# A hybrid decoder layer in float32: other pairs of products in the down projection, its sums on VectorE, and float32 sums at the FFN's entry

## The chip, the core and the metric

One core of one Trainium2 chip runs the whole layer in one launch. The metric is the time of the program on the device in microseconds (us). Of the core's engines, TensorE (PE) multiplies matrices into PSUM, VectorE (DVE) and ScalarE (ACT) work on SBUF and PSUM, GpSimd (POOL) on SBUF, and SyncE (SP) issues most of the transfers (DMA), in its program's order.

## What is computed

The reference is one layer over x, 1024 tokens of 1024 features, all in float32: a mixer of pooling and gated linear attention, an attention over 256 memory tokens, and a feed-forward network (FFN) with a causal convolution of width 3, each added to the residual, with a final norm. The change lies in the last part:

```python
h = rms_norm(x, norm_ffn_w)
u = h @ w_up                       # 1024 x 5632
u = conv_b + conv_w[0]*u_pad[:, 0:s] + conv_w[1]*u_pad[:, 1:1+s] + conv_w[2]*u_pad[:, 2:2+s]
x = x + (silu(u[..., :2816]) * u[..., 2816:]) @ w_down
return rms_norm(x, norm_final_w)
```

## The kernel before

**Three products for one.** Every float32 factor is held as a pair: `hi`, a copy rounded by ScalarE (L96, for weights L117), and `lo`, what is left, subtracted by VectorE (L97, L118). A product of two factors is three matmuls, hi·hi, lo·hi and hi·lo (`mm3c`, L888 to L892), of 128 x 128 by 128 x 512. A pair for the next product is called a unit.

**Seven block products for eight.** Both matrix products of the FFN cut their factors into two by two blocks and form seven products of sums of blocks. For the up projection the two halves of the tokens and of the features are the blocks, and the sums of activations are T1 to T4 and B22; for the down projection the two halves of 2816 inner features (11 blocks `k` of 128 each) and of 1024 outputs.

**The entry of the FFN.** Before the up projection, eight tiles of 128 tokens are normed (`normed`, L297) and transposed on TensorE (L829). The first four become pairs in H3. Of the other four `sums12` (L822) forms T1, T2 and B22, and `sums34` (L838) T3 and T4, out of the pairs: `whole` (L806) has GpSimd add hi and lo again (L811), and VectorE subtracts (L815). This runs beside the end of the attention's output projection and the first up jobs. `up_units` (L914) prepares the weight units of one of 22 blocks `f`, with sums of weights on GpSimd (L880, L883). The first three blocks are begun with two products each (`up_pre`, L949), then `up` (L967) does the other five; later blocks do all seven, 84 matmuls.

**The down projection** (`down`, L1083) goes over the 11 blocks k four times: products 1 and 2 in pass one, 6 and 5 in pass two, 3 and 7 in pass three, 4 in pass four. Each product of one k is four token tiles of three matmuls (`run`), so a pass has 264 matmuls, the fourth 132. Units come from `feed`, pass by pass; `take` keeps five of them ready. `units12` to `units4` load the gated activations (`G`, spilled to DRAM, as is the residual) and weights, form sums on GpSimd (`padd`, `psub`) or VectorE (`less`), and split them. Pass four loads its weights again (`wpair`). Finished sums go onto the residual R: the sums of one set of PSUM banks by VectorE (L877), the others by `spread`, a ScalarE copy and a GpSimd addition. During pass four the tiles 0 to 3 are normed and stored (L1128); the last two k of pass four run tile by tile, and tiles 4 to 7 are normed behind them, half by half (L1143 to L1150).

**What sets the order.** A scheduler fixes each engine's order of instructions when the program is built; SP's queue takes loads and stores in that order, and an instruction that waits holds all behind it on its engine. Buffers come from pools: two for raw weights of the down projection, four for hi and lo of units and eight more among the big ones, five and three PSUM banks.

Of the kernel before, what the change touches and what calls it, by code (L numbers as in the profile page):

```python
# [15 lines left out]
P = 128  # L16
# [26 lines left out]
def hybrid_layer(ctx: ExitStack, tc: tile.TileContext, x, mem, norm_mix_w, w_in, pool_w, pool_scale,  # L43
# [754 lines left out]

    for t in range(4):
        spill(t)  # L800
    finish(J["wo", 1, 0])
    B22 = Feat(TB, HK)
    for i in (1, 2):
        TT[i] = Feat(TB, HK)

    def whole(feat, k0, c0):  # L806

        r = t2(512).rearrange("p (k c) -> p k c", k=HK)
        for j in (0, 2):
            h = feat.slot(k0 + j)[:, :, c0:c0 + P]  # L810
            pin(nc.gpsimd.tensor_tensor(r[:, j:j + 2, :], h.hi.bitcast(F32), h.lo.bitcast(F32), ALU.add))  # L811
        return r

    def less(dst, a, b):
        nc.vector.tensor_tensor(dst, a, b, ALU.subtract)  # L815

    def tquad():
        return t2(512).rearrange("p (k c) -> p k c", k=HK)

    def sums12(xn, i, b11):  # L822

        c0 = i * P
        ps = []
        for q in range(2):
            p = bankB()
            for j in range(4):
                nc.tensor.transpose(p[:, j * P:(j + 1) * P], xn[:, (4 * q + j) * P:(4 * q + j + 1) * P], ident)  # L829
            ps.append(p.rearrange("p (k c) -> p k c", k=HK))  # L830
        less(b11, ps[0], b11)
        t = tquad()
        less(t, ps[1], b11)
        B22.put(0, HK, c0, P, ps[1])
        TT[2].put(0, HK, c0, P, t)
        TT[1].put(0, HK, c0, P, b11)

    def sums34(i):  # L838
        c0 = i * P
        t, b = whole(TT[2], 0, c0), whole(H3, 0, c0)  # L840
        less(b, t, b)
        TT[3].put(0, HK, c0, P, b)
        b = whole(H3, HK, c0)
        less(b, b, t)
        TT[4].put(0, HK, c0, P, b)

    plan[0].open = True
    b1 = whole(H3, 0, 0)
# [51 lines left out]
    def b11(k):  # L900
        return H3.k(k)
# [301 lines left out]
```

## Time and profile before

| | |
|---|---|
| median of three runs | 1356.41 us (1355.82 to 1357.3) |
| the profiled run | 1357.08 us, of which its span 1355.3 us |
| mean granted TensorE clock of the span | 0.978 of full |
| busy: TensorE, VectorE, ScalarE, GpSimd | 1288.3, 881.9, 640.5, 372.6 us |
| instructions: VectorE, ScalarE, GpSimd | 1248, 1150, 341 |
| moved by DMA | 149.71 MB, mean 110 GB/s |

The trace is of one execution. The views used are the stretches (busy time of each engine in stretches of the span, with granted clock), and the timeline (instructions in order of time, equal neighbours merged as x2, with the idle time ahead and what ended it). Matmuls are pipelined: a row's duration is longer than the distance of two starts. Pass one begins at 1084.24 us, pass two at 1147.60, pass three at 1233.54, pass four at 1296.07.

### The profile page before, as it was taken

The page shows a single profiled execution, that of the slowest core. Times are in us where ns is not written, and L with a number is a line of the kernel's source. Part 1 is how long each engine was busy: PE and PEld are TensorE (multiplying, and loading weights), DVE is VectorE, ACT ScalarE, POOL GpSimd, SP SyncE. Part 2 cuts the span into 40 slices and gives each one's busy share as a digit, 9 for nine tenths or more (in the row PEclk, how much of TensorE's full clock was granted, in tenths as well). Part 3 has the DMA queues.
Part 4 walks back from the last instruction along what each step waited for, and adds up shares of the span by engine and source line. Part 5 has one row for each costly group of instructions (what it writes and reads, how often), then busy time and mean ns, then how long its engine had stood idle before and what let it go on. Part 6 is the DMA issues. An engine that isn't in the chain of part 4 may idle for free. (4 is left out here: it accounts for less than half of the span.)

```text
span 1355.3 us, 17032 instructions
## 1 busy us (share of the span) xinstructions
PE 1288.3 (95%) x6326; PEld 1068.6 (79%) x6326; DVE 881.9 (65%) x1248; ACT 640.5 (47%) x1150; POOL 372.6 (27%) x341
## 2 busy tenths in 40 slices
PE   8999999999999999999789999999999999788975
PEld 7898878888778899988568888888888877676853
DVE  6623765237666544477877667766776674999565
ACT  6536444364455433354355545554555454234443
POOL 2000110001200000024844433444344302764273
PEclk9999999999999999999799999999999999899988
DMA  9333134322322222243123222222222477433333
GB/s 294 125 95 91 63 133 160 94 71 73 141 78 63 63 66 75 91 136 117 47 79 102 68 94 93 71 70 94 94 70 71 155 272 269 164 110 112 106 128 120
DMA packets 143521, 149.71 MB, mean 110 GB/s; under 512 B 4744, under 2 KB 112974, under 8 KB 143439
## 3 DMA queue, kind: packets, MB, share of 16 engines
q1 hardware_dynamic: 142431, 146.02, 33.5%
q0 software_dynamic: 432, 1.57, 0.4%
q8 instruction: 49, 0.80, 0.2%
q10 hardware_dynamic: 576, 1.05, 0.2%
q14 instruction: 33, 0.27, 0.1%
HBM read 128.70 MB, written 19.92 MB: 110 GB/s over the span
## 5 line engine op out<-in xcount | busy, mean ns | idle before, releaser
L118 DVE TENSOR_TENSOR wl<-wr,wh 128x512 fp32r<-128x512 f32 (+1 forms) x222 | 155.7, 702 | 209.6 <-ACT wh L117 204.9
L117 ACT ACTIVATE wh<-wr 128x512 fp32r<-128x512 f32 (+1 forms) x222 | 140.2, 632 | 285.8 <-PE pa L91 82.1
L890 PE MATMUL pa<-r,wh 128*128 128x512 f32 x400 | 159.6, 399 | 5.2 <-ACT f L886 5.2
L90 PE MATMUL pa<-wh,r 128*128 128x512 f32 (+2 forms) x480 | 159.1, 332 | 0.0
L891 PE MATMUL pa<-r,wh 128*128 128x512 f32 x400 | 158.9, 397 | 0.0
L892 PE MATMUL pa<-r,wl 128*128 128x512 f32 x400 | 158.2, 396 | 0.1
L92 PE MATMUL pa<-wh,r 128*128 128x512 f32 (+2 forms) x480 | 157.0, 327 | 0.2
L91 PE MATMUL pa<-wl,r 128*128 128x512 f32 (+2 forms) x480 | 157.2, 327 | 0.0
L90 PE MATMUL pa<-r,wh 128*128 128x512 f32 (+1 forms) x384 | 150.1, 391 | 0.7 <-ACT r L96 0.7
L92 PE MATMUL pa<-r,wl 128*128 128x512 f32 (+1 forms) x384 | 144.7, 377 | 0.3 <-DVE wl L118 0.3
L91 PE MATMUL pa<-r,wh 128*128 128x512 f32 (+1 forms) x384 | 144.6, 377 | 0.0
L92 PEld LDWEIGHTS pa<-wh,r 128*128 128x128 f32 x480 | 90.3, 188 | 9.4 <-DVE r L97 1.0
L90 PEld LDWEIGHTS pa<-wh,r 128*128 128x128 f32 x480 | 90.4, 188 | 7.8 <-ACT r L96 0.2
L91 PEld LDWEIGHTS pa<-wl,r 128*128 128x128 f32 x480 | 90.4, 188 | 7.7 <-issue 0.2
L963 DVE SCALAR_TENSOR_TENSOR f<-f,vec,f 128x1023 f32<-128x1023 f32 x44 | 86.8, 1975 | 14.5 <-ACT f L962 14.5
L890 PEld LDWEIGHTS pa<-r,wh 128*128 128x128 f32 x400 | 76.3, 191 | 25.2 <-ACT f L886 7.9
L117 ACT ACTIVATE wh<-ws 128x512 fp32r<-128x512 f32 x88 | 55.3, 629 | 80.4 <-PE pa L891 33.9
L892 PEld LDWEIGHTS pa<-r,wl 128*128 128x128 f32 x400 | 76.1, 190 | 17.9 <-DVE wl L118 0.4
L891 PEld LDWEIGHTS pa<-r,wh 128*128 128x128 f32 x400 | 76.2, 190 | 16.8
L892 PE MATMUL pb<-r,wl 128*128 128x512 f32 x216 | 85.9, 398 | 3.6 <-DVE wl L118 3.6
L890 PE MATMUL pb<-r,wh 128*128 128x512 f32 x216 | 86.1, 399 | 3.3 <-ACT wh L117 3.0
L891 PE MATMUL pb<-r,wh 128*128 128x512 f32 x216 | 85.9, 398 | 0.0
(215 smaller groups left out, 2828.8 us busy)
## 6 DMA issues: line engine op xcount, KB each, us to landing
wr<-in_ffn_w_up_dram SPq DMA_DIRECT2D x47, 512.0 KB, 3.7
wr<-in_ffn_w_down_dram SPq DMA_DIRECT2D x44, 512.0 KB, 4.2
wr<-in_w_in_dram SPq DMA_DIRECT2D x24, 512.0 KB, 4.0
gd<-f SPq DMA_DIRECT2D x22, 512.0 KB, 2.6
f<-gd SPq DMA_DIRECT2D x22, 512.0 KB, 5.8
f<-in_xattn_wkv_dram SPq DMA_DIRECT2D x16, 512.0 KB, 7.1
f<-in_x_dram SPq DMA_DIRECT2D x16, 512.0 KB, 7.3
wr<-in_w_out_dram SPq DMA_DIRECT2D x16, 512.0 KB, 3.6
```

The lines of the kernel that those rows point to most:

```text
L90: nc.tensor.matmul(ps, l.hi, r.hi, start=start, stop=False)
L91: nc.tensor.matmul(ps, l.hi, r.lo, start=False, stop=False)
L92: nc.tensor.matmul(ps, l.lo, r.hi, start=False, stop=stop)
L117: ia = nc.scalar.activation(w.hi, src, AF.Copy)
L118: ib = nc.vector.tensor_tensor(w.lo, src, w.hi.bitcast(F32), ALU.subtract)
L890: nc.tensor.matmul(ps, l.hi, r.hi, start=start, stop=False, **kw)
L891: nc.tensor.matmul(ps, l.hi, r.lo, start=False, stop=False, **kw)
L892: nc.tensor.matmul(ps, l.lo, r.hi, start=False, stop=stop, **kw)
L963: nc.vector.scalar_tensor_tensor(v[:, 1:], u[:, 0:T - 1], cw(1, f), v[:, 1:], ALU.mult, ALU.add)
```

## The change

**The FFN's entry.** A class `Blocks` takes the place of H3 and TT. The first four tiles' transposes become pairs, and ScalarE also copies them to SBUF in float32 (`half0`). The other four tiles' sums are formed from these copies and from PSUM by VectorE alone, in one pass per tile (`half1`); GpSimd adds no hi and lo any more. The pairs of T1, T3, B22 and T4 are split one name at a time over all four tiles (`split`). The up projection's weight sums of blocks 0 and 1 move from GpSimd to VectorE. The norm's 1/1024 goes into ScalarE's square.

**The down projection.** Passes are 1 and 5, 6 and 3, 7 and 2, then 4. All sums are VectorE's; GpSimd has none, and ScalarE one copy per k in pass two. Pass four loads and sums nothing: its operand is left over from pass three. Each set of banks is added to the residual by VectorE straight from PSUM (`onto`), at the end of every pass, and banks are used on. Two more buffers hold raw weights. The loads of the residual move into pass one, after k=5. The last four k, instead of two, run tile by tile, and in the final norm the sum of the two squares is one GpSimd addition with the small constant added by VectorE.

```diff
 def up_units(f, part):
+    q = nc.vector if f < 2 else nc.gpsimd
-    padd(st[1], st[21], st[22])
+    q.tensor_tensor(st[1], st[21], st[22], ALU.add)
...
-def sums12(xn, i, b11):
-def sums34(i):
+    def half0(self, i, xn):
+        r = f4(2, 512)
+        self.raw["T3", i], self.raw["T4", i] = r[:, 0], r[:, 1]
+        for q, p in enumerate(self.rows_T(xn)):
+            self.first.put(4 * q, 4, i * P, P, quad(p))
+            copy(r[:, q], p)
+    def half1(self, i, xn):
+        b12, b22 = self.rows_T(xn)
...
+        less(r[:, 0], b12, t3)
+        less(t, b22, r[:, 0])
+        self.done["T2"].put(0, HK, i * P, P, quad(t))
+        copy(r[:, 1], b22)
+        less(t3, t, t3)
+        less(t4, t4, t)
...
+def units15(k):
+    less(b12, b12, b11)
+    add(s1, g1[:, 1, :], g2[:, 1, :])
+    less(g1[:, 1, :], g1[:, 0, :], g1[:, 1, :])
+    less(g1[:, 0, :], g2[:, 1, :], g1[:, 1, :])
+def units63(k):
+    less(b12, b22, b12)
+    add(b12, b12, b11)
+    less(s4, g2[:, 0, :], g1[:, 0, :])
+    nc.scalar.activation(g1[:, 0, :], b12, AF.Copy)
+def units72(k):
+    less(b11, g1[:, 0, :], b11)
+    less(g1[:, 0, :], b21, g1[:, 0, :])
 def units4(k):
-    b11, b21 = wpair(k, 0)
-    psub(b21, b21, b11)
-    less(b21, b21, g1[:, 0, :])
-    yield unit(g2[:, 1, :]), unit(b21)
+    yield unit(a2[k][:, 1, :]), unit(a1[k][:, 0, :])
...
+    def onto(t0, hs, ps):
+        for t in range(4):
+            add(R[t0 + t][:, hs], ps[t], R[t0 + t][:, hs])
+    X, Y = banks(), banks()
+    yield from both(X, Y, True, True, residual)
+    onto(0, lo, X)
+    onto(4, hi, Y)
+    yield from both(X, Y, False, False)
+    onto(0, hi, X)
+    onto(0, hi, Y)
+    Z = banks()
+    yield from both(X, Z, False, True)
+    onto(4, hi, X)
+    onto(0, lo, Z)
+    for k in range(KH - LAST):
+        yield from run(X, False, False)
```

**Three places in the order.** In the rows below a line number, an operation and its tiles stand for each instruction; numbers behind a tile's letter tell one tile from another.

VectorE at the entry, where the last tile of tokens is summed, before. `wl` are the lo parts of weight units (the first two rows those of block 1), `r` lo parts of activations; L815 are sums:

```order
L118 TENSOR_TENSOR wl_6188<-wr_6185,wh_6187 128x512
L118 TENSOR_TENSOR wl_6192<-wr_6185,wh_6191 128x512
L815 TENSOR_TENSOR t_6138<-pb_6221,t_6138 128x512 [waits PE_49]
L118 TENSOR_TENSOR wl_6297<-wr_6294,wh_6296 128x512 [waits DMAHW2_49]
L815 TENSOR_TENSOR t_6232<-pb_6226,t_6138 128x512 [waits DVE_49,PE_49]
L97 TENSOR_TENSOR r_5881<-t_6138,r_5879 128x2x128 [waits Activation_49]
L97 TENSOR_TENSOR r_5882<-t_6138,r_5880 128x2x128 [waits Activation_49]
L97 TENSOR_TENSOR r_5877<-pb_6226,r_5875 128x2x128 [waits Activation_49]
L97 TENSOR_TENSOR r_5885<-t_6232,r_5883 128x2x128 [waits DVE_49,Activation_49]
L97 TENSOR_TENSOR r_5886<-t_6232,r_5884 128x2x128 [waits Activation_49]
L97 TENSOR_TENSOR r_5878<-pb_6226,r_5876 128x2x128 [waits Activation_49]
```

There the units of block 1 stand ahead of the last tile's sums. After, L800 are the sums, and the four lo parts `wl` at the end are those of blocks 1 and 2:

```order
L97 TENSOR_TENSOR r_6307<-f_5956,r_6305 128x2x128 [waits DMAHW2_49,Activation_49]
L800 TENSOR_TENSOR f_5814<-t_6216,f_5814 128x512 [waits DVE_49]
L97 TENSOR_TENSOR r_5944<-t_6216,r_5942 128x2x128 [waits Activation_49]
L97 TENSOR_TENSOR r_5945<-t_6216,r_5943 128x2x128 [waits Activation_49]
L800 TENSOR_TENSOR f_5814<-f_5814,t_6216 128x512
L97 TENSOR_TENSOR r_6306<-f_6037,r_6304 128x2x128
L97 TENSOR_TENSOR r_6307<-f_6037,r_6305 128x2x128
L97 TENSOR_TENSOR r_6306<-f_6114,r_6304 128x2x128
L118 TENSOR_TENSOR wl_6172<-wr_6169,wh_6171 128x512 [waits DMAHW7_49,Activation_49]
L118 TENSOR_TENSOR wl_6176<-wr_6169,wh_6175 128x512 [waits Activation_49]
L118 TENSOR_TENSOR wl_6231<-wr_6228,wh_6230 128x512 [waits DMAHW1_49,Activation_49]
L118 TENSOR_TENSOR wl_6247<-wr_6228,wh_6246 128x512 [waits Activation_49]
```

The lo parts of T1 (r_6306, r_6307) and the last tile's sums stand ahead of block 1's units now.

VectorE at the change from pass one to pass two, before; L877 adds PSUM banks (`pa`) onto the residual, L815 are sums, L97 lo parts:

```order
L97 TENSOR_TENSOR wl_10091<-wr_10056,wh_10090 128x512 [waits DMAHW5_49,PE_49,Activation_49]
L877 TENSOR_TENSOR f_10106<-pa_9610,f_10106 128x512 [waits DMAHW6_49,PE_49,Pool_49]
L877 TENSOR_TENSOR f_10108<-pa_9611,f_10108 128x512 [waits DMAHW7_49,PE_49,Pool_49]
L877 TENSOR_TENSOR f_10110<-pa_9612,f_10110 128x512 [waits DMAHW0_49,PE_49,Pool_49]
L877 TENSOR_TENSOR f_10112<-pa_9613,f_10112 128x512 [waits DMAHW1_49,PE_49,Pool_49]
L815 TENSOR_TENSOR f_9620<-f_9620 128x512 [waits Pool_49]
L815 TENSOR_TENSOR f_9620<-ds_10144,f_9620 128x512 [waits DVE_49]
L815 TENSOR_TENSOR f_9621<-f_9621,f_9620 128x512 [waits DVE_49]
L97 TENSOR_TENSOR r_10152<-f_9620,r_10152 128x512 [waits Activation_49]
```

After, L803 with `pa` or `pb` adds a PSUM bank, L803 with `wr` a sum of weights, L97 are lo parts of k=1:

```order
L803 TENSOR_TENSOR wr_10102<-wr_10102 128x512 [waits DVE_49]
L97 TENSOR_TENSOR wl_10111<-f_9534,wh_10110 128x512 [waits PE_49]
L803 TENSOR_TENSOR f_9895<-pb_9587,f_9895 128x512 [waits PE_49]
L97 TENSOR_TENSOR wl_10115<-wr_10102,wh_10114 128x512 [waits Activation_49]
L97 TENSOR_TENSOR wl_10132<-t_10105,wh_10131 128x512 [waits Activation_49]
L97 TENSOR_TENSOR wl_10136<-t_10104,wh_10135 128x512 [waits Activation_49]
L803 TENSOR_TENSOR f_9897<-pb_9588,f_9897 128x512 [waits PE_49]
L803 TENSOR_TENSOR f_9899<-pb_9589,f_9899 128x512 [waits PE_49]
L803 TENSOR_TENSOR f_9901<-pa_9590,f_9901 128x512 [waits PE_49]
```

Eight banks (four X, four Y) are added there, not four, with three lo parts after the first; sums that waited for GpSimd are gone from behind them.

SP's queue around the stores of the normed tiles (L1128), before:

```order
L274 DMA wr_11207<-in_ffn_w_down_dram 128x2x512 [waits DMAHW6_49,DVE_49,Pool_49]
L1128 DMA out_dram<-f_11150 128x1024 [waits DVE_49]
L1128 DMA out_dram<-f_11158 128x1024 [waits DVE_49]
L1128 DMA out_dram<-f_11166 128x1024 [waits DVE_49]
L1128 DMA out_dram<-f_11174 128x1024 [waits DVE_49]
L274 DMA wr_11232<-in_ffn_w_down_dram 128x2x512 [waits DMAHW7_49,DVE_49,Pool_49]
L274 DMA wr_11259<-in_ffn_w_down_dram 128x2x512 [waits DMAHW0_49,DVE_49,Pool_49]
L274 DMA wr_11286<-in_ffn_w_down_dram 128x2x512 [waits DMAHW5_49,DVE_49,Pool_49]
L274 DMA wr_11308<-in_ffn_w_down_dram 128x2x512 [waits DMAHW6_49,DVE_49,Pool_49]
```

After (L1144 are these stores, L1164 those of the last tiles):

```order
L274 DMA wr_10918<-in_ffn_w_down_dram 128x2x512 [waits DMAHW4_49,DVE_49]
L274 DMA wr_10962<-in_ffn_w_down_dram 128x2x512 [waits DMAHW5_49,DMAHW1_49,DVE_49]
L274 DMA wr_11002<-in_ffn_w_down_dram 128x2x512 [waits DMAHW6_49,DVE_49]
L1144 DMA out_dram<-f_11148 128x1024 [waits DVE_49]
L1144 DMA out_dram<-f_11178 128x1024 [waits DVE_49]
L1144 DMA out_dram<-f_11210 128x1024 [waits DVE_49]
L1144 DMA out_dram<-f_11242 128x1024 [waits DVE_49]
L1164 DMA out_dram<-f_9903 128x512 [waits DMAHW0_49,DVE_49]
```

No load stands behind the four stores any more, and those ahead of them are pass three's.


## Rows read from the trace of the kernel before

**Rows 1.** The page, part 2: granted TensorE clock in 40 equal slices.

```profile
PEclk9999999999999999999799999999999999899988
```

**Rows 2.** Stretches of 34 us: busy PE, PEld, DVE, ACT, POOL (instructions), clock, DMA share, GB/s.

```profile
646.00:680.00 34.00, 25.59 (x88) 18.23 (x87) 29.50 (x38) 11.30 (x28) 26.22 (x24) 0.80 0.17 49
...
1050.00:1084.00 34.00, 34.00 (x149) 27.69 (x148) 21.62 (x25) 15.00 (x24) 10.31 (x7) 1.00 0.45 155
...
1084.00:1118.00 34.00, 31.86 (x137) 25.23 (x136) 24.70 (x36) 18.28 (x30) 1.54 (x1) 1.00 0.75 269
...
1186.00:1220.00 34.00, 30.57 (x122) 24.12 (x121) 34.00 (x32) 11.25 (x21) 23.75 (x15) 0.93 0.36 109
...
1288.00:1322.00 34.00, 24.64 (x101) 19.44 (x100) 22.87 (x22) 13.68 (x29) 25.45 (x21) 0.85 0.37 135
```

**Rows 3.** Timeline of TensorE: start us, us, line, operation [idle <-releaser]; first up block to last.

```profile
632.61 0.47 PE L890 MATMUL pa<-r,wh 128*128 128x512 f32 x1
...
716.03 0.39 PE L890 MATMUL pa<-r,wh 128*128 128x512 f32 x1
...
1084.24 0.39 PE L890 MATMUL pb<-wh,wh 128*128 128x512 f32 x1
...
1147.60 0.39 PE L890 MATMUL pb<-r,r 128*128 128x512 f32 x1
...
1233.54 0.50 PE L890 MATMUL pa<-r,r 128*128 128x512 f32 x1 [3.64 <-DVE f L877]
...
1296.07 0.40 PE L890 MATMUL pb<-wh,wh 128*128 128x512 f32 x1
...
1342.93 0.39 PE L892 MATMUL pa<-r,r 128*128 128x512 f32 x1
```

**Rows 4.** Timeline of TensorE behind four of its waits.

```profile
662.40 0.80 PE L892 MATMUL pb<-r,wl 128*128 128x512 f32 x1 [3.57 <-DVE wl L118]
...
1155.19 0.79 PE L890 MATMUL pa<-r,r 128*128 128x512 f32 x1 [3.45 <-DVE f L877]
...
1159.62 0.55 PE L890 MATMUL pa<-r,r 128*128 128x512 f32 x1
...
1317.17 0.80 PE L891 MATMUL pb<-r,r 128*128 128x512 f32 x1 [8.99 <-DVE r L97]
```

**Rows 5.** Timeline of VectorE (DVE): entry, start of pass one, start of pass two.

```profile
631.25 0.74 DVE L97 TENSOR_TENSOR r<-t,r 128x256 fp32r<-128x256 f32 x2
...
655.94 5.28 DVE L97 TENSOR_TENSOR r<-t,r 128x256 fp32r<-128x256 f32 x6
...
1086.20 0.69 DVE L97 TENSOR_TENSOR wl<-wr,wh 128x512 fp32r<-128x512 f32 x1
...
1086.81 0.69 DVE L97 TENSOR_TENSOR r<-f,r 128x512 fp32r<-128x512 f32 x1
...
1088.61 2.47 DVE L963 SCALAR_TENSOR_TENSOR f<-f,vec,f 128x1023 f32<-128x1023 f32 x2
...
1154.46 2.47 DVE L877 TENSOR_TENSOR f<-pa,f 128x512 f32<-128x512 f32 x4
...
1161.96 1.77 DVE L815 TENSOR_TENSOR f<-f 128x512 f32<-128x512 f32 x1 [1.19 <-POOL ds L880]
```

**Rows 6.** Timeline of GpSimd (POOL) in pass two.

```profile
1161.88 1.30 POOL L883 TENSOR_TENSOR ds<-ds,wr 128x512 f32<-128x512 f32 x1
```

**Rows 7.** Timeline in pass four: VectorE, then SP's queue (issue of transfers).

```profile
1311.50 2.28 DVE L299 SCALAR_TENSOR_TENSOR f<-f,s,f 128x1024 f32<-128x1024 f32 x1 [0.44 <-POOL s L294]
...
1306.47 7.67 SPq L1128 DMA_DIRECT2D out_dram<-f  x4
...
1317.18 15.30 SPq L274 DMA_DIRECT2D wr<-in_ffn_w_down_dram  x5
```

**Rows 8.** Timeline of GpSimd and ScalarE (ACT) at the last tile.

```profile
1349.38 0.59 POOL L1145 TENSOR_SCALAR s<-s 128x1 f32<-128x1 f32 x1
...
1350.65 0.72 ACT L1148 ACTIVATE f<-f,s 128x512 f32<-128x512 f32 x1 [0.61 <-POOL s L1146]
```

More of the change, by code (lines that the diff above doesn't have):

```diff
@@ L789, in hybrid_layer @@
     wb_f = bcast_row(norm_ffn_w)
-    H3 = Feat(TB)
-    weave(norm_feat([lambda i=i: xres[i] for i in range(4)], wb_f, H3))
-    TT = {}
+    first.close()
+    ypool = ExitStack()
+    ybuf = ypool.enter_context(tc.tile_pool(name="ybuf", bufs=2))
     dram = ctx.enter_context(tc.tile_pool(name="dram", bufs=1, space=bass.MemoryType.DRAM))
@@ L952, in gen @@
             x, z = bankA(), bankA() if f < 2 else bankB()
-            yield from product(x, b11, True)
-            yield from product(z, b21, True)
+            yield from product(x, HB["B11"], True)
+            yield from product(z, HB["B21"], True)
             begun[f] = x, z
@@ L974, in gen @@
                 x = bankU()
-                yield from product(x, b11, True)
+                yield from product(x, HB["B11"], True)
             sa, ug = f4(2, TB), f4(2, TB)
@@ L1026, in unit @@
             w = Pair(t[:, 0, :], t[:, 1, :])
[L1027 removed]
+        nunit[0] += 1
         split(w, src)
         return w
[L1031 to L1042 removed]
+    def units15(k):
+        g1, g2 = a1[k], a2[k] = f4(2, TB), f4(2, TB)
+        dma(g1, G[k])
+        b11, b12 = raw_down(wd[k, :, 0, :], True)
+        dma(g2, G[KH + k])
+        yield unit(g1[:, 0, :]), unit(b11)
+        less(b12, b12, b11)
+        s1 = t2(512)
+        add(s1, g1[:, 1, :], g2[:, 1, :])
+        less(g1[:, 1, :], g1[:, 0, :], g1[:, 1, :])
+        yield unit(s1), unit(b12)
+        less(g1[:, 0, :], g2[:, 1, :], g1[:, 1, :])
@@ L1073, in hybrid_layer @@
+    def units4(k):
+        yield unit(a2[k][:, 1, :]), unit(a1[k][:, 0, :])
+    feed = (u for us in (units15, units63, units72, units4) for k in range(KH) for u in us(k))
     ready = []
@@ L1081, in take @@
         return ready.pop(0)
+    LAST = 4
     def down():
@@ L1091, in run @@
                 yield 0.7
-        def spread(r, ps):
-            s = t2(512)
-            copy(s, ps)
-            padd(r, s, r)
-        X, Z = banks(), banks()
-        for k in range(KH):
-            yield from run(X, k == 0, k == KH - 1)
-            yield from run(Z, k == 0, k == KH - 1)
-        for t in range(8):
-            R[t] = f4(D)
-            dma(R[t], XS[t])
-        for t in range(4):
-            spread(R[t][:, 0:512], X[t])
-        for t in range(4):
-            add(R[t][:, 0:512], Z[t], R[t][:, 0:512])
@@ L1109, in down @@
-        turn[0] += 4
-        Y = banks()
-        for k in range(KH):
-            for ps, fresh in ((Y, k == 0), (X, False)) if k == KH - 1 else ((X, False), (Y, k == 0)):
-                yield from run(ps, fresh, k == KH - 1)
-        for t in range(4):
-            add(R[4 + t][:, 512:], Y[t], R[4 + t][:, 512:])
-        for t in range(4):
-            spread(R[t][:, 512:], X[t])
-        wb = bcast_row(norm_final_w)
-        for k in range(KH):
-            for ps in (X, Y) if k == KH - 1 else (Y, X):
-                yield from run(ps, False, k == KH - 1)
@@ L1122, in down, with both @@
-        for t in range(4):
-            spread(R[4 + t][:, 512:], X[t])
-        for t in range(4):
-            add(R[t][:, 512:], Y[t], R[t][:, 512:])
+        def both(U, V, fu, fv, mid=None):
+            for k in range(KH):
+                yield from run(U, fu and k == 0, k == KH - 1)
+                yield from run(V, fv and k == 0, k == KH - 1)
+                if mid and k == 5:
+                    mid()
+        lo, hi = slice(0, 512), slice(512, D)
+        def onto(t0, hs, ps):
+            for t in range(4):
+                add(R[t0 + t][:, hs], ps[t], R[t0 + t][:, hs])
@@ new lines, in residual @@
+        def residual():
+            for t in range(8):
+                R[t] = f4(D)
+                dma(R[t], XS[t])
+        X, Y = banks(), banks()
[5 more added lines that the diff above has]
+        onto(0, hi, Y)
+        turn[0] += 4
+        Z = banks()
+        wb = bcast_row(norm_final_w)
+        yield from both(X, Z, False, True)
+        onto(4, hi, X)
+        onto(0, lo, Z)
```

231 lines of the change are left out of this document (101 added, 130 removed).

## The prediction

> **What bounds the kernel now.** I read the stretches first, then TensorE's rows in time order, then the engines that it waits for. In a middle stretch TensorE is busy 34.00 of 34.00 us at clock 1.00 [rows 2], and nothing on another engine can matter there. Over the span the clock falls below nine tenths only in slices 20, 35, 39 and 40 [rows 1]. So the time to win lies at the entry of the FFN and in the down projection, and I sized it by counting matmuls. A pass of two products has 264 (11 k, four token tiles, two products, three matmuls each) and the fourth, of one product, 132. At the pace of the middle stretch, 149 in 34.00 us [rows 2], these are 60.2 and 30.1 us. Before, the four passes take 63.4, 85.9, 62.5 and 46.8 us, and 12.4 us follow from the last matmul's start to the end of the span [rows 3]. The losses are 3.2, 25.7, 2.3, 16.7. At the entry, the 252 matmuls of the first three blocks stand between 632.61 and 716.03 [rows 3]; at that pace they take 57.5 of 83.4 us, and with about 1 for the eight transposes among them some 25 are lost.
>
> Where TensorE sat idle, rows name the releaser: DVE wl of a weight unit at the entry, DVE f L877 and DVE lo parts in pass two, and 8.99 us for DVE r L97 in pass four [rows 4]. Each long wait is paid twice: behind the 3.45 us wait matmuls show 0.63 us where the same form shows 0.39 [rows 3, 4]; the mean granted clock of such stretches is 0.80, 0.93 or 0.85 [rows 2], a mixture of the full 2.4 GHz and the half of it. From 1155.19 to 1159.62 eleven rows take 4.43 us, at full clock 2.5: I count 1.9 for each new long wait.
>
> Why VectorE is late in pass two: it is busy 34.00 of 34.00 us with only 32 instructions [rows 2], 1.06 us each. The same 128x512 subtraction takes 0.69 us, one starting 0.60 after another, where GpSimd is idle, and 1.77 while a GpSimd sum of the same size runs from 1161.88 on [rows 5, 6]. Additions that read PSUM take 2.47 us for four, 0.62 each [rows 5]. So the sums on GpSimd are dear through what they do to VectorE.
>
> **The change, part by part.** The count of matmuls stays the same, so each part is priced by the wait it takes or gives.
>
> Second pass (6+3 for 6+5). VectorE has three sums and four lo parts per k before and after; GpSimd's three sums per k go and become one of those. 7 x 0.60 = 4.2 us per k stands against 5.48 of TensorE (60.2 / 11), and VectorE gains on it. All the loss but the handover from pass one should go. That handover stands in the second place of the order: after the first PSUM add, three lo parts of unit k=1 lie ahead of the adds of X's other banks, which TensorE wants at once. X's last matmuls end 2.7 us before the pass does (12 x 0.23), and four adds and four lo parts are 4.8: 2.1 us of wait, and up to 1.9 more at half clock. Pass two: 60.2 + 3.5 = 63.7, **gain 22** (15 to 24).
>
> First pass (1+5 for 1+2). Its lo parts stay four per k, and four sums are new: 8 x 0.60 = 4.8 us against 5.48. Cover is 0.7 per k, no more. It starts with VectorE's last convolution in front: four three-operand operations of 2.47 us a pair [rows 5] and a product of 1.2, some 6 us, while TensorE needs k=1's second unit about 8 us in; with k=1's own sums behind them I take a wait of 2 to 4 us plus 1.9. The residual loads, eight of 512 KB, now lie in this pass, in front of the last three pairs of G. Transfers were busy 0.75 of the time there [rows 2], and removed loads come from other passes; their cover is the five units kept ready, and if that fails it costs 1 to 4 us. Bounds are a gain of 3 (before's 3.2 of loss goes, nothing new comes) and a loss of 6.5 (60.2 + 5.9 + 4 against 63.4); I take 60.2 + 4.9 + 1.8 = 66.9, **loss 3.5**.
>
> Third pass (7+2 for 3+7). Two sums and four lo parts per k are 3.6 us, and no GpSimd sum is left. Eight PSUM adds at its start wait for TensorE, but the units of k=0 and k=1 are ahead of them in VectorE's queue. Loss before was 2.3; I take **no change** (2 gained to 3 lost).
>
> Fourth pass. The 8.99 us wait ended with a lo part that stood on VectorE behind all four norm products, each waiting for GpSimd's small operations among its sums; the last ran from 1311.50 for 2.28 us [rows 4, 7]. SP's queue held five weight loads behind the four stores (1306.47, 7.67 us), the next went out at 1317.18 [rows 7], and every unit after that waited for load, GpSimd and VectorE in a row. After it no weight is loaded in this pass and none is summed (third place of the order), its second operand was left in SBUF by pass three, and the norm tiles come one per k. What then could be late are the lo parts of units 5 to 8, each behind a norm tile: 1.2 for the product (the pair of three-operand operations in [rows 5]), 0.6 for the weight multiplication, and GpSimd's two small operations, near 0.6 to 1.3 us each. Per unit VectorE spends about 3.1 us, TensorE 2.74, and four units are ready before. So 30.1 + 0 to 5 us: 32.5, **gain 14** (9 to 16).
>
> Tail. Tiles now end 2.74 us apart, not 1.37, so the last tile finds its engines free. From its last matmul: 0.4 + add 0.7 + square 0.8 + GpSimd's add and power, 0.6 to 1.0 each, + scale 0.72 [rows 8] + 0.4 between them + 4 for the store (before, 1355.3 - 1351.4 = 3.9 after the last scaling): 8.2 to 9. **Gain 3.5** (1 to 5).
>
> Entry. GpSimd's sums of hi and lo go, f=0 and f=1 weight sums move to VectorE. Six 128x256 lo parts took 5.28 us beside them, 0.88 each, where two of them took 0.74 without [rows 5]. The wait for the norm of the last tile then goes, as its product stood behind those lo parts. What takes its place is in the first order: f=1's units lie behind the lo parts of T1. Five sums of 0.60 and eight lo parts of 0.37 stand there after the tile's transposes, with their hi parts on ScalarE at the same pace, about 6 us, of which some 2 are covered by f=0's products: 4.5 us of wait (an estimate from those rows) and 1.9 of half clock. I add 6 for the other units of f=1 and f=2, a quarter of what before loses, since f=2's sums are still on GpSimd and ScalarE's hi parts stand in front. Loss 12.4 for 25, **gain 12** (6 to 18).
>
> Other edits, nothing: from f=2 on the up jobs are unchanged, and TensorE hides their 34.00 of 34.00 and the square with a scale is as many operations as before.
>
> The sum against the profiled run: 12 - 3.5 + 22 + 0 + 14 + 3.5 = 48 us, 1357.1 - 48 = **1309** (that run's span is 1355.3, 1.8 lie around it, and it is 0.7 above the median of three).
>
> **Rivals.** *VectorE becomes the bound of pass one.* If its operations follow each other at their duration, 0.69 and not 0.60 us, eight are 5.5 per k, as much as TensorE's 5.48. The 6 us of convolution are then never made up, and every handover finds VectorE's queue behind: pass one 69, and two handovers at 4 more each with half clock, 1319. For it speaks that each lo part waits for ScalarE; against it the rows with starts 0.61 apart at 0.69 each [rows 5]. Chance 0.13. The Trainium skill ("VectorE: DVE Perf Modes", section "The DRAIN you can't avoid") says just this: the next operation does not start until the pipe is empty, and leaving out waits does not help. By that rule the result would be this rival's 1319. The trace disagrees here, with starts 0.09 us ahead of the previous end, so it keeps a small chance.
>
> *Transfers hold pass one.* The residual's 4 MB stand in front of the last pairs of G in SP's queue, in a stretch where 269 GB/s were moved [rows 2]. At that rate they take 15.6 us, and a queue that is 10 us behind at the end of the pass would cost 10 with half clock: 1321. Against it, five units are kept ready, and the last pass gives its 11 loads up. Chance 0.06.
>
> *The waits move, they don't go.* Entry keeps its 25 (f=1's units wait longer behind T1), and the handovers cost 5 each: 1357 - 36 + 10 = 1331. Chance 0.08.
>
> *VectorE stays slow, and the kernel gets slower.* The place is the three passes with sums; the price is set by 8, 7 and 6 VectorE operations per k, 231 in all, against TensorE's 181 us. If VectorE's 1.77 us came from TensorE's reads or from transfers and not from GpSimd, the entry would win nothing, and the three passes would last as long as VectorE. They took 211.8 before, pass four and the tail still give 17.5, so it is slower than before from 229 us on, a mean of 0.99 us per operation. At pass two's 1.06 they last 245: 1357 + 16 = 1373. Against it: in pass one transfers were at 0.75 and TensorE at 31.86 of 34, and yet rows there show 0.69 [rows 2, 5]. Chance 0.03.
>
> **How the numbers follow.** The forecast has 0.70. The bounds of its parts all at once would give 1289 and 1336 (gains of 68 and 21.5); they don't fail together, and its own range is 1295 to 1324. The first three rivals lie at 1319 to 1331. So the range is 1293 to 1332; left out are the slower case and the far ends. What a measurement of this kernel tells from no change is about 0.2%, 2.7 us. Faster 0.96, same 0.01, slower 0.03.
>
> **What would show it.** Right: in the profile after, GpSimd has no sums in the passes; VectorE's 128x512 operations are all 0.69, never 1.7; pass two lasts 62 to 65 us; no TensorE wait above 1 us stands in pass four; 8 to 9 us follow the last matmul. Wrong: TensorE waits for DVE r or wl inside pass one at every k (first rival), for a G load (second), above 6 us near 640 (third), or VectorE full at above 0.8 us each without GpSimd (fourth).

## The result, and the profile after

The changed kernel takes 1310.91 us, the median of four runs (1310.09 to 1311.38), against 1356.54 (1355.82 to 1357.3) before: a ratio of 0.9663 (95%: 0.9646 to 0.968). The forecast was 1309. The total is right to 2 us, but errors of both signs cancel in it, as the stages show. The profiled run took 1311.38 us with a span of 1309.4; before, 1357.08 with 1355.3.

| stage | before | after | gained | forecast (bounds) |
|---|---|---|---|---|
| entry, to block 3 | 83.4 | 68.9 | 13.5 (it starts 1.0 later) | 12 (6 to 18) |
| blocks 3 to 21 | 368.2 | 368.2 | 0 | 0 |
| pass one | 63.4 | 77.8 | -14.5 | -3.5 (+3 to -6.5) |
| pass two | 85.9 | 61.4 | 24.5 | 22 (15 to 24) |
| pass three | 62.5 | 60.3 | 2.3 | 0 (2 to -3) |
| pass four | 46.9 | 30.0 | 16.8 | 14 (9 to 16) |
| from the last matmul | 12.4 | 9.2 | 3.2 | 3.5 (1 to 5) |

The gains add up to 45.8, the spans differ by 45.9. A wait at a change of passes counts in the pass before, as a pass ends with the next one's first matmul. The stage limits are TensorE's rows that answer to [rows 3]; in the timeline of after, the first of the up projection, of block 3, of the four passes, and the last matmul:

```profile
633.58 0.47 PE L911 MATMUL pa<-r,wh 128*128 128x512 f32 x1
...
702.49 0.40 PE L911 MATMUL pa<-r,wh 128*128 128x512 f32 x1
...
1070.70 0.87 PE L911 MATMUL pb<-wh,wh 128*128 128x512 f32 x3
...
1148.52 0.47 PE L911 MATMUL pb<-r,r 128*128 128x512 f32 x1 [1.56 <-ACT wh L96]
...
1209.95 0.39 PE L911 MATMUL pb<-r,r 128*128 128x512 f32 x1
...
1270.21 0.40 PE L911 MATMUL pb<-wh,wh 128*128 128x512 f32 x1
...
1300.24 0.39 PE L913 MATMUL pa<-r,r 128*128 128x512 f32 x1
```

The page of after, granted clock in 40 slices (answers to [rows 1]). Before, slices 20, 35, 39 and 40 fell below nine tenths; now it is slice 35 alone, from 1113.0 to 1145.7 us, and that is the end of pass one:

```profile
PEclk9999999999999999999999999999999999899999
```

Stretches of after, as in [rows 2] (busy PE, PEld, DVE, ACT, POOL with instructions, clock, DMA share, GB/s): the end of pass one and the middle of pass two.

```profile
1102.00:1136.00 34.00, 26.11 (x103) 20.62 (x102) 22.59 (x38) 11.31 (x20) 0.00 (x0) 0.85 0.90 350
...
1170.00:1204.00 34.00, 34.00 (x151) 27.96 (x150) 33.05 (x56) 19.03 (x35) 0.00 (x0) 1.00 0.43 141
```

Pass two is now TensorE's: 34.00 of 34.00 us. VectorE does 56 instructions in 33.05 us, 0.59 each, where it did 32 in 34.00, 1.06 each [rows 2]. At the end of pass one TensorE is busy for only 26.11 of 34 at clock 0.85, transfers for 0.90 at 350 GB/s, and GpSimd does nothing at all.

The five largest waits of TensorE in after from 600 us on, summed by who ended them (us in total, times, longest):

```profile
PE pb L911 <- ACT r L96: 7.9, 1, 7.9
PE pa L911 <- ACT wh L117: 4.6, 1, 4.6
PE pa L911 <- ACT r L96: 2.6, 1, 2.6
PE pa L911 <- ACT f L806: 2.5, 3, 1.3
PE pb L911 <- ACT wh L96: 1.6, 1, 1.6
```

None lies in pass three or four. The longest is in pass one: TensorE stands still for 7.9 us. ScalarE is only the messenger there, as the timeline of SP's queue and of ScalarE shows:

```profile
1110.71 4.10 SPq L274 DMA_DIRECT2D f<-xd  x8
1115.35 2.36 SPq L274 DMA_DIRECT2D f<-gd  x2
...
1119.94 4.11 SPq L274 DMA_DIRECT2D f<-gd  x4
...
1126.30 0.63 ACT L96 ACTIVATE r<-f 128x512 fp32r<-128x512 f32 x1 [12.44 <-DMA f<-gd]
...
1127.50 0.79 PE L911 MATMUL pb<-r,r 128*128 128x512 f32 x1 [7.87 <-ACT r L96]
```

Eight tiles of the residual (`xd`) go out first, 4 MB, then a pair of `G` (`gd`) that TensorE lacks from 1119.63 (1127.50 less 7.87). It was issued at 1115.35 and landed at 1126.3. The transfers' view of 1108 to 1130 us (count, size, median us to landing) shows how long such a pair took; over the whole run of after that landing is 8.1 us:

```profile
f<-gd SPq DMA_DIRECT2D x6, 512.0 KB, 10.6
```

In these 22 us 8.02 MB were moved. Behind the wait the matmuls show 0.79 us where 0.39 is usual, as in [rows 4], at the lower of the clock's two levels. The two k around it (k=7 and 8) took 13.5 and 8.3 us where 5.48 is the pace: 10.8 us lost.

### The profile page after: what moved, and what is told of

The parts are those of the page before. It is cut to its first block, busy times and chain, and to the rows that moved or that the text cites. A ratio compares the mean times of both kernels' runs of the same rounds, so it can differ in the third digit from the quotient of the medians.

```text
span 1309.4 us, 16875 instructions
## 1 busy us (share of the span) xinstructions
PE 1271.6 (97%) x6326; PEld 1062.3 (81%) x6326; DVE 864.9 (66%) x1331; ACT 644.8 (49%) x1161; POOL 221.2 (17%) x230
## 4 chain that ended last, share of the span: by engine, by line
PE 83%; issue 5%; DVE 5%; DMA 4%; ACT 2%; POOL 1%; SPq 0%; POOLq 0%; ACTq 0%; DVEq 0%
PE pa L90 11%; PE pa L92 11%; PE pa L91 11%; PE pa L911 9%; PE pa L912 9%; PE pa L913 9%; PE pb L911 5%; PE pb L912 5%; PE pb L913 5%; DMA f<-gd 1%; PE pb L307 1%; DVE r L97 1%; DMA wr<-in_ffn_w_up_dram 1%; DVE wl L118 1%; DVE wl L97 1%
## 5 line engine op out<-in xcount | busy, mean ns | idle before, releaser
L118 DVE TENSOR_TENSOR wl<-wr,wh 128x512 fp32r<-128x512 f32 (+1 forms) x222 | 152.9, 691 | 208.6 <-ACT wh L117 203.5
L911 PEld LDWEIGHTS pa<-r,wh 128*128 128x128 f32 x400 | 75.6, 189 | 26.0 <-ACT wh L117 4.8
L979 DVE SCALAR_TENSOR_TENSOR f<-f,vec,f 128x1023 f32<-128x1023 f32 x44 | 86.8, 1974 | 14.5 <-ACT f L978 14.5
L912 PEld LDWEIGHTS pa<-r,wh 128*128 128x128 f32 x400 | 75.7, 189 | 16.7
L90 PEld LDWEIGHTS pa<-r,wh 128*128 128x128 f32 x384 | 73.2, 191 | 14.8 <-issue 1.6
```

The source lines that it names most:

```text
L90: nc.tensor.matmul(ps, l.hi, r.hi, start=start, stop=False)
L118: ib = nc.vector.tensor_tensor(w.lo, src, w.hi.bitcast(F32), ALU.subtract)
L911: nc.tensor.matmul(ps, l.hi, r.hi, start=start, stop=False, **kw)
L912: nc.tensor.matmul(ps, l.hi, r.lo, start=False, stop=False, **kw)
L979: nc.vector.scalar_tensor_tensor(v[:, 1:], u[:, 0:T - 1], cw(1, f), v[:, 1:], ALU.mult, ALU.add)
```

## The experiments

Ratios are to the kernel before. The edits are to the kernel after, unless said otherwise; `...` marks lines left out.

### What holds pass one

*Theory:* the residual's loads in front of `G` cost pass one some 10 us, and with them out of the way pass one comes out near the forecast's 67. *Rival:* VectorE has no slack there, and the wait comes back elsewhere.

**residual_after**: the loads where pass one is done.

```diff
-        yield from both(X, Y, True, True, residual)
+        yield from both(X, Y, True, True)
+        residual()
```

> The kernel after, with the residual loads behind pass one's last k, as in the kernel before. Theory: pass one falls to 66 to 69 us, but the eight tiles now come 5 to 10 us too late for the additions from PSUM that stand at the start of pass two, and TensorE waits there for DVE adds: 1305 to 1312 us in all, a wait moved and not taken away. Rival (the loads have nothing to do with pass one's wait): pass one stays above 75 us.

Measured: 1305.34 us (1304.73 to 1306.28), ratio 0.9619 (0.9602 to 0.9635). Pass one took 70.9 us, pass two 62.9. The 7.9 us wait is gone, pass one missed the 66 to 69 expected, and a new wait stands at the change to pass two:

```profile
1142.16 0.77 PE L911 MATMUL pb<-r,r 128*128 128x512 f32 x1 [5.14 <-DVE f L803]
```

The expectation put it down to a residual that comes too late for the additions. VectorE's timeline doesn't bear that out: from 1125.49 us to the last addition its operations follow each other without idle time, so the additions waited for VectorE's own queue.

**residual_spread**: one tile after each of k=1 to 8, in the same pass.

```diff
-                if mid and k == 5:
-                    mid()
+                if mid and 1 <= k <= 8:
+                    mid(k - 1)
...
```

> The kernel after, with one change: pass one loads one residual tile after each of k=1 to 8, instead of all eight after k=5. Theory (eight loads of 512 KB in a row stand in SP's queue ahead of G's pairs for k=8 to 10, and these come late): the 7.9 us wait of TensorE at 1127.5 and the half clock around it go, pass one lasts 66 to 69 us instead of 77.8, and the kernel 1300 to 1303 us. Rival (pass one moves as much as the queues can carry, wherever the loads stand): the same wait comes in smaller parts, pass one stays at 75 to 79 and the kernel within 3 us of 1310.9. Rival (VectorE with eight operations per k is the bound): the same, with TensorE waiting for DVE lo parts at every k.

Measured: 1308.47 us (1307.45 to 1309.27), ratio 0.9643 (0.9624 to 0.9663); pass one 73.0, pass two 61.9. Missed: the wait is gone, but k=2 to 9 of pass one take 5.6 to 6.8 us, and TensorE waits for 4.4 us at 1144.11. The bytes are the same, so spreading the loads gives back only a part, and the ratio's interval overlaps that of after.

**residual_halves**: of each residual tile only the half that pass one's sums go to is loaded in pass one (one per k), the other half in pass two.

```diff
+        def residual1(k):
+            if 1 <= k <= 8:
+                R[k - 1] = f4(D)
+                part(k - 1, lo if k <= 4 else hi)
+        def residual2(k):
+            if 1 <= k <= 8:
+                part(k - 1, hi if k <= 4 else lo)
...
```

> The kernel after, with residual tiles loaded by halves, one half after each of k=1 to 8: in pass one the eight halves that are added at its end, in pass two the others. Theory (what pass one moves within its time is what counts, and it has 2.1 MB less to move): neither the 7.9 us wait in pass one nor the 4 to 5 us one at its end, pass one 66 to 69 us with the wait behind the last convolution left, pass two 61 to 63, the kernel 1299 to 1304 us. Rival (VectorE's eight operations per k leave no room to make up the start's delay): a wait of 3 to 5 us stays at the end of pass one, as with whole tiles spread, and the kernel is at 1304 to 1309.

Measured: 1307.42 us (1305.91 to 1309.02), ratio 0.9642 (0.9626 to 0.9658); pass one 72.0, pass two 62.5, and 3.83 us for `DVE f L803` at the change. The rival's outcome.

**late_halves**: the same halves, but those of pass one are issued together after k=8, behind the last of `G` (the edit is to residual_halves).

```diff
         def residual1(k):
-            if 1 <= k <= 8:
-                R[k - 1] = f4(D)
-                part(k - 1, lo if k <= 4 else hi)
+            if k == 8:
+                for t in range(8):
+                    R[t] = f4(D)
+                    part(t, lo if t < 4 else hi)
```

> The kernel after, with eight half tiles of the residual (those added at pass one's end, 2.1 MB) loaded after k=8 of pass one, behind G's last pairs, and the other halves one by one in pass two. Theory (two things cost pass one's end: the residual in front of G, or the residual late for the additions): both waits go, the 7.9 us one of the kernel after and most of the 5.1 us one of the kernel that loads behind pass one; pass one 65 to 68 us, pass two 61 to 63, the kernel 1299 to 1303 us. Rival (VectorE has eight operations per k and nothing in hand at the end of pass one): a wait of 3 to 5 us for VectorE's additions stays, 1304 to 1307 us.

Measured: 1303.74 us (1303.53 to 1306.91), ratio 0.9616 (0.9602 to 0.963): below the kernel after (its interval, 0.9646 to 0.968, lies apart) by some 7 us. The interval overlaps those of residual_after and late_conv, so these three can't be ranked. Pass one 68.7, pass two 62.1: together 130.8, where the forecast had 66.9 + 63.7 = 130.6. What still stands is a wait of 3.41 us at the change of passes. Stretches of this kernel in pass one, the last of them all of pass one, and VectorE's timeline in front of that wait:

```profile
1090.00:1110.00 20.00, 20.00 (x89) 16.37 (x88) 19.43 (x32) 9.11 (x17) 0.00 (x0) 1.00 0.86 331
1110.00:1130.00 20.00, 20.00 (x89) 16.35 (x88) 18.66 (x32) 9.16 (x18) 0.00 (x0) 1.00 0.74 275
1130.00:1150.00 20.00, 16.59 (x66) 13.11 (x65) 19.98 (x35) 8.43 (x16) 0.00 (x0) 0.91 0.99 340
...
1071.77:1140.52 68.75, 62.62 (x266) 50.30 (x264) 66.11 (x104) 33.46 (x57) 0.00 (x0) 0.98 0.77 282
```

```profile
1137.28 0.68 DVE L97 TENSOR_TENSOR r<-wr,r 128x512 fp32r<-128x512 f32 x1
1137.88 0.68 DVE L97 TENSOR_TENSOR r<-t,r 128x512 fp32r<-128x512 f32 x1
1138.49 0.68 DVE L97 TENSOR_TENSOR wl<-t,wh 128x512 fp32r<-128x512 f32 x1
1139.09 0.68 DVE L97 TENSOR_TENSOR r<-t,r 128x512 fp32r<-128x512 f32 x1
1139.69 1.88 DVE L803 TENSOR_TENSOR f<-pb,f 128x512 f32<-128x512 f32 x3
...
1140.52 0.48 PE L911 MATMUL pb<-r,r 128*128 128x512 f32 x1 [3.41 <-DVE f L803]
```

VectorE is busy for 19.43, 18.66 and 19.98 of 20 us while TensorE still runs at full pace for the first two, and over the whole pass for 66.11 us, where TensorE's matmuls need 60.2. The additions that free the banks begin at 1139.69, behind a row of lo parts without a gap, and TensorE had been out of work since 1137.1. The first set of banks was finished at 1134.4, and nine VectorE operations on pass two's units stand between that and the additions. No run put the additions ahead of them, so how much of the wait is VectorE's load and how much is this order stays open.

**ahead4**: four units, not three, made ready before pass one begins, so that k=1 stands ahead of the last convolution.

```diff
-                down_ahead(3)
+                down_ahead(4)
```

> The kernel after, with four instead of three units of the down projection made within the last up job, so that the sums and lo parts of k=1's second unit stand ahead of the last convolution in VectorE's queue. Theory (TensorE's wait of 2.6 us at 1081.8 comes from the convolution's four operations in front of that unit): this wait and its half clock go, 4 us; but pass one then reaches its late loads earlier, and the 7.9 us wait grows by what was gained: 1308 to 1311 us. Rival (the wait at 1081.8 has another cause, a load of G): it stays, and nothing changes.

Measured: 1311.2 us (1309.79 to 1312.09), ratio 0.9668 (0.9654 to 0.9682). Missed: the first wait of pass one only moved, from 1081.77 (2.58 us) to 1085.51 (2.50), and the one for `G` is 8.19.

**late_conv**: late_halves, and the last convolution with its product put off until after k=2 of pass one.

```diff
...
+            if k == 2:
+                late[0]()
...
```

> The kernel late_halves, and the second half of the last convolution with its gate product put off until after k=2 of pass one (its result is loaded again only for k=10). Theory (the convolution's operations in front of k=1's unit cost the 2.6 us wait and half clock at pass one's start, 4.4 us): that loss goes, 1295 to 1299 us. Rival (VectorE is the bound of pass one as a whole, so that what is moved comes back at its end): within 2 us of late_halves.

Measured: 1304.87 us (1302.41 to 1305.6), ratio 0.9615 (0.9601 to 0.9629): no gain over late_halves. k=1 takes 6.0 us, not 10.0, but two short waits (0.68 and 0.90 us) come up in the middle, and the one at the change of passes, ended by `DVE f L803`, grows from 3.41 to 5.64. VectorE is busy for 66.06 us of this pass one and for 66.11 of late_halves'. So with the loads out of the way the runs agree with VectorE as the bound of pass one as a whole, with the 6 us of convolution that it starts with: what is moved within the pass returns by its end.

### What a sum on GpSimd costs

**pass2_sums_pool**: pass two's three sums per k on GpSimd, all else as after.

```diff
-        less(b12, b22, b12)
-        add(b12, b12, b11)
-        less(s4, g2[:, 0, :], g1[:, 0, :])
+        nc.gpsimd.tensor_tensor(b12, b22, b12, ALU.subtract)
+        nc.gpsimd.tensor_tensor(b12, b12, b11, ALU.add)
+        nc.gpsimd.tensor_tensor(s4, g2[:, 0, :], g1[:, 0, :], ALU.subtract)
```

> The kernel after, with the three sums of pass two (6+3) on GpSimd instead of VectorE; all else as it is. Theory (a GpSimd operation with SBUF operands holds a VectorE operation with two SBUF operands, 1.77 us instead of 0.69): VectorE has only four lo parts per k left, yet three of its operations per k take 1.3 to 1.8 us; pass two lasts 68 to 80 us instead of 61.4 and the kernel 1318 to 1330. Rival (GpSimd only did too much work in a chain before, contention does no harm): with 3 x 1.3 us = 3.9 per k GpSimd keeps pace with 5.5, VectorE is relieved of 1.8 us per k, and pass two stays at 60 to 63 us.

Measured: 1329.06 us (1328.37 to 1330.45), ratio 0.9794 (0.9777 to 0.9812). Pass two takes 77.3 us instead of 61.4, its end included (9.75 us for `DVE f L803` at 1225.27). A stretch of its pass two, then VectorE and GpSimd:

```profile
1165.00:1185.00 20.00, 20.00 (x90) 16.48 (x89) 20.00 (x16) 7.52 (x14) 16.67 (x11) 1.00 0.54 162
```

```profile
1173.07 0.68 DVE L97 TENSOR_TENSOR r<-f,r 128x512 fp32r<-128x512 f32 x1
1173.67 1.78 DVE L97 TENSOR_TENSOR r<-wr,r 128x512 fp32r<-128x512 f32 x1
...
1173.22 1.68 POOL L1069 TENSOR_TENSOR t<-f,f 128x512 f32<-128x512 f32 x1 [0.63 <-DVE wl L97]
```

VectorE loses three sums per k and gets later by it: 16 instructions fill its 20 us, 1.25 each. GpSimd is not full, at 16.67 of 20 us.

**before_sums_dve**: the kernel before, with the down projection's sums on VectorE and its pairs as they were.

```diff
-        padd(x, g1[:, 1, :], g2[:, 1, :])
+        add(x, g1[:, 1, :], g2[:, 1, :])
...
-        psub(b11, b12, b11)
-        psub(b22, b22, b11)
+        less(b11, b12, b11)
+        less(b22, b22, b11)
...
-        psub(g1[:, 0, :], b22, b12)
+        less(g1[:, 0, :], b22, b12)
...
-        psub(b21, b21, b11)
+        less(b21, b21, b11)
```

> The kernel before, with the sums of the down projection's units moved from GpSimd to VectorE in passes two, three and four; pairs of products, loads and additions onto the residual are unchanged. Theory (contention): pass two has ten VectorE operations per k, 10 x 0.60 = 6.0 us, more than the 5.48 of TensorE, so VectorE paces it at 66 to 71 us instead of 85.9 although VectorE was busy all of the time before; pass three 61 to 64; pass four 41 to 46 with its loads still late; the kernel 1332 to 1343. Rival (VectorE's time per operation does not come from GpSimd): ten operations of 1.06 us are 10.6 per k, pass two lasts 115 us and the kernel is slower than 1356.5.

Measured: 1328.63 us (1327.42 to 1330.71), ratio 0.9791 (0.9772 to 0.981). Pass two falls from 85.9 to 64.5 us, pass four from 46.9 to 40.3; passes one and three stay within 1.4. So the move of the sums alone is 28 of the 45.6 us, 21.4 of the 24.5 in pass two, but 6.6 of the 16.8 in pass four; no run takes the other 10.2 apart. Better than expected, in passes two and four. Its first matmuls of passes two and three, and a stretch between them:

```profile
1147.21 0.39 PE L890 MATMUL pb<-r,r 128*128 128x512 f32 x1
...
1211.71 0.39 PE L890 MATMUL pb<-r,r 128*128 128x512 f32 x1
```

```profile
1150.00:1205.00 55.00, 52.17 (x224) 41.74 (x224) 54.82 (x87) 22.41 (x40) 3.86 (x3) 1.00 0.54 180
```

VectorE does more work per k than before, and does it at 0.63 us each, not 1.06.

**junk_read**: six additions of 128x256 that nothing needs, per k of pass three, on GpSimd. **junk_write**: the five in the loop are memsets of the same size.

```diff
         less(b11, g1[:, 0, :], b11)
+        nc.gpsimd.tensor_tensor(jt[0], b11[:, 0:256], b11[:, 0:256], ALU.subtract)
+        for _ in range(5):
+            nc.gpsimd.tensor_tensor(jt[0], jt[0], jt[0], ALU.add)
...
```

> The kernel after, with six GpSimd operations of 128x256 per k added to pass three that feed nothing there (each reads SBUF twice; one begins on a weight sum, five on its own result; the last result, zero, is added to a norm's sum). Theory (a GpSimd operation that reads SBUF holds VectorE's two-input operations): VectorE's 128x512 operations in pass three, 0.69 us in the kernel after, show 1.0 to 1.4 us where they meet one, and pass three lasts 62 to 80 us instead of 60.3. Rival (contention needs long operations or particular tiles): 0.69 us and 60.3 us as before.

> As junk_read, but five of the six operations per k only write: memset of the same 128x256 tile. Theory (reading is what collides; the Trainium skill, page "SBUF — State Buffer", section "Who interferes with whom", says that a VectorE instruction with two SBUF inputs contends with a GpSimd one that reads SBUF, not with one that only writes): VectorE's operations stay at 0.69 us beside the memsets and are longer only beside the one reading operation per k; pass three 60 to 61 us. Rival (any GpSimd operation on SBUF collides): as junk_read.

Measured, one run each: 1316.42 and 1311.64 us. Pass three takes 61.3 and 60.3 us: for junk_read that is below the 62 to 80 expected, though VectorE's operations are as long as expected, and TensorE waits for 2.31 us for its additions at 1214.05, counted in pass two. Timeline of VectorE, then of GpSimd, in junk_read at the change to pass three:

```profile
1213.31 1.87 DVE L803 TENSOR_TENSOR f<-pb,f 128x512 f32<-128x512 f32 x3
1215.11 3.06 DVE L803 TENSOR_TENSOR f<-pa,f 128x512 f32<-128x512 f32 x5
...
1218.70 1.10 DVE L97 TENSOR_TENSOR wl<-wr,wh 128x512 fp32r<-128x512 f32 x1
...
1212.92 3.70 POOL L1082 TENSOR_TENSOR jt<-jt 128x256 f32<-128x256 f32 x5
...
1217.39 4.92 POOL L1082 TENSOR_TENSOR jt<-jt 128x256 f32<-128x256 f32 x5
```

And in junk_write:

```profile
1228.60 1.10 DVE L97 TENSOR_TENSOR wl<-f,wh 128x512 fp32r<-128x512 f32 x1
1229.63 0.68 DVE L97 TENSOR_TENSOR wl<-wr,wh 128x512 fp32r<-128x512 f32 x1
...
1228.10 1.06 POOL L1080 TENSOR_TENSOR jt<-wr 128x256 f32<-128x256 f32 x1 [3.26 <-DVE wr L800]
1229.22 1.79 POOL L1082 MEMSET jt<- 128x256 f32 x5
```

A subtraction with both operands in SBUF takes 1.10 us while GpSimd reads, and 0.68 while GpSimd only writes. An addition with one operand in PSUM isn't held up: the eight from 1213.31 on last 4.9 us in all, 0.6 each, beside GpSimd's additions. The Trainium skill ("SBUF — State Buffer", section "Who interferes with whom") says just this: VectorE's second SBUF input comes through a read path that it shares with GpSimd, so it contends with a GpSimd instruction that reads SBUF and not with one that only writes. The traces agree: 0.68 us against 1.10 (half-size reads) and 1.78 (full-size reads).

### The entry and the tail

**up_load_slot**: the up projection's raw weights get another buffer for block 1. In after, TensorE waits for 4.60 us at 644.79; the chain of what ended last shows, in order of time (start, us):

```profile
639.32 0.89 PE pb L825 x8
...
640.22 3.80 DMA wr<-in_ffn_w_up_dram
...
644.11 0.64 ACT wh L117
```

The load goes out the moment the last transposes end (L825), 640.21. By the program its buffer lies in memory that the pool of normed tiles had, and these transposes read the last of them; SP's queue waits there for TensorE's L825.

```diff
-    raws = [1]
+    raws = [0]
```

> The kernel after, with the counter that deals raw up-projection weights to buffers begun at 0 instead of 1, so that block 1's first load gets one of the two old buffers and block 2's the new one. Theory (that load had to wait until the transposes of the last token tile had read the norm pool's memory, which the new buffer takes over: issued at 640.22, TensorE's wait of 4.6 us ended at 644.79 behind it): block 1's units are ready in time, the 4.6 us wait goes or shrinks to under 1.5 us for block 2's unit, and the kernel takes 1304 to 1308 us. Rival (the forecast's reason: VectorE's and ScalarE's parts of T1 stand ahead of block 1's units): the wait stays at 4 to 5 us and the kernel at 1309 to 1312.

Measured: 1313.78 us (1313.43 to 1315.29), ratio 0.969 (0.9676 to 0.9705). Missed: that wait is gone, but the kernel is no faster (the ratio's interval overlaps that of after), and the entry takes 68.5 us for 68.9. TensorE waits for 3.18 us a little later, for hi parts whose sums stand behind lo parts of T1 and T3 that VectorE does in one run:

```profile
648.06 9.81 DVE L97 TENSOR_TENSOR r<-f,r 128x256 fp32r<-128x256 f32 x29
...
660.46 0.54 PE L911 MATMUL pb<-r,wh 128*128 128x512 f32 x1 [3.18 <-ACT wh L117]
```

**last2**: two k tile by tile at the end, as before the change, not four.

```diff
-    LAST = 4
+    LAST = 2
```

> The kernel after, with two instead of four last k run tile by tile. Theory (the tail is shorter since tiles end 2.74 us apart and each chain of add, square, power and scaling finds its engines free): 11.5 to 13 us instead of 9.2 follow the last matmul, and the kernel takes 1313 to 1315 us. Rival (the tail is shorter because of the other edits of the final norm): 9 to 10 us, 1310 to 1312.

Measured: 1314.17 us (1312.13 to 1315.44), ratio 0.9689 (0.9675 to 0.9704). From the last matmul's start to the end of the span it is 11.2 us instead of 9.2, so 2.0 of the tail's 3.2 come from the four k. This is read from the traces; the ratios' intervals overlap.

## Why the prediction was right, and where it was not

**What bound the kernel.** Right. The four passes needed 60.2 us each (30.1 the last) by the count of matmuls, and passes three and four now take 60.3 and 30.0.

**Why VectorE was late.** Right, and now shown by four runs: it was slow through GpSimd's reads. The sums moved back in pass two cost 15.8 us there; moved alone in the kernel before they give 21.4; added reads slow VectorE's SBUF subtractions from 0.68 to 1.10 us, and writes don't. Of the prediction's signs, pass two came out just below its 62 to 65 us, and the second rival's sign of being wrong, a TensorE wait for a `G` load in pass one, did appear.

**Pass one: the step that failed.** The term was a loss of 3.5 us, and it was 14.5, outside its bounds. The first part of that step stands: forecast were 4.9 us for the convolution in front, and k=1 took 9.9 us, 4.4 above pace. VectorE's timeline has what was counted, four three-operand operations in two pairs:

```profile
1075.07 2.47 DVE L979 SCALAR_TENSOR_TENSOR f<-f,vec,f 128x1023 f32<-128x1023 f32 x2
1077.46 2.47 DVE L980 SCALAR_TENSOR_TENSOR f<-f,vec,f 128x1022 f32<-128x1022 f32 x2
...
1080.45 1.22 DVE L1016 TENSOR_TENSOR f<-f,f 128x1024 f32<-128x1024 f32 x1
```

The second part, "their cover is the five units kept ready, and if that fails it costs 1 to 4 us", was mis-sized: 1.8 us in the sum, 10.8 measured. Five units are two and a half k, 13.7 us at 5.48, and I set that against the residual as if `G` were issued that far ahead. It was issued 4.3 us before TensorE ran dry (1115.35 against 1119.63), and behind 4 MB of residual it took 10.6 us to land. The rival that named this ("transfers hold pass one", 10 with half clock) had mechanism and price right; I gave it 0.06, as a case of its own, when it belonged in the sum. (Its total, 1321, lies 12 above the forecast; with 10.8 in place of the 1.8 already counted it is 1318.) The five kernels that move those loads all lose this wait. The other 2.4 us lie mainly in the last k, with the 1.56 us wait at the change of passes. Without the loads in front of `G` pass one is 68.7 to 73.0 us, and in late_halves passes one and two together are what the forecast had.

**VectorE as the bound of pass one.** This rival's premise fell and half of its conclusion came true. Operations follow each other at 0.60, not 0.69: VectorE's timeline in pass two of after, 56 of them in 33.05 us:

```profile
1171.16 0.68 DVE L800 TENSOR_TENSOR wr<-t,wr 128x512 f32<-128x512 f32 x1
1171.76 0.69 DVE L800 TENSOR_TENSOR t<-f,f 128x512 f32<-128x512 f32 x1
1172.37 0.69 DVE L803 TENSOR_TENSOR wr<-wr 128x512 f32<-128x512 f32 x1
```

The rule of the Trainium skill named with it ("VectorE: DVE Perf Modes", section "The DRAIN you can't avoid") says that the next operation does not start until the pipe is empty, and adds that one which is not held starts earlier. These rows go with the addition and not with the rule as the rival took it: each starts 0.08 us before the one ahead ends. Yet at 0.60 too, eight per k and pass two's first sums leave too little room for the convolution, as the 66.1 us of VectorE in late_halves and late_conv show. In the kernel after this is hidden: TensorE loses 10.8 us on `G`, and the handover shows 1.56 us. Once the loads are out of the way, 3.4 to 5.6 us appear there, in all five kernels that tried. The forecast's 2.1 + 1.9 for that handover, put into pass two, was about right in size for these, not for after.

**Passes two, three and four** gained 2.5, 2.3 and 2.8 us more than forecast, each just above its bound. For pass two I kept 3.5 us for the handover; after has 1.56 us of it, counted in pass one, and a wait of 0.7 behind it. In pass four no TensorE wait is left, so the lo parts behind the norm tiles never were late. Before's loss in pass three (2.3) lies in its first k, 7.7 us for 5.48, behind the 3.64 us wait at 1233.54 [rows 3]; after has no such wait. It is not the GpSimd sum: before_sums_dve has that sum on VectorE, and its pass three takes 63.9 us.

**Entry.** The size was right (13.5 for 12, a first wait of 4.60 for 4.5), the reason was not. I had VectorE's lo parts of T1 ahead of block 1's weights; it was the load of these weights, held by memory that the transposes still read. VectorE's queue was next in line: with the load freed, a wait came back at 660 behind the lo parts that the forecast had named. What each edit at the entry gave was not taken apart by a run.

**Tail.** Right: 3.2 for 3.5, with 9.2 us behind the last matmul where 8.2 to 9 were worked out.

**The total** was right because pass one's miss of 11 us met 9.1 us of small gains beyond the forecast (1.5 + 2.5 + 2.3 + 2.8). That it came within 2 us is luck, and no proof of the sum.

## What to carry to other kernels

Price a sum on GpSimd by what it does to VectorE's SBUF-to-SBUF operations beside it, not by its own time. Where a change moves loads into another pass, add up that pass's bytes and look when the next needed load is issued in the queue, against how long it takes to land behind them; a count of buffers says nothing on that. Where an engine has hardly any slack over a whole stage, taking one wait away can bring another up at the stage's end: pass one lost 17.6 us (77.8 less 60.2), and six edits there made the kernel faster by 0 to 7 us, three of them clear of noise.

## What the runs showed of the hardware

- GpSimd and VectorE hold each other up: GpSimd's 128x512 sum, 1.29 us where VectorE is idle (before, at 1137.83), takes 1.62 to 1.75 in pass2_sums_pool from 1165 to 1185 us, and VectorE's 0.68 becomes 1.78. In the junk runs VectorE was held up only with two operands in SBUF, and only while GpSimd read SBUF.
- Transfers reached a mean of 364 GB/s over 22 us in pass one of after (8.02 MB); a 512 KB load of `G` then took 10.6 us to land instead of the 5.8 that was the median before.
- TensorE at 34.00 of 34.00 us and 0.43 of transfers left VectorE's pace untouched (0.59 us each, in pass two of after).
